# Squares for the FFN's 1/rms through PSUM and VectorE, and plain weight blocks multiplied ahead of the sums

## The chip, the cores and the metric

The kernel runs on one core of one Trainium2 chip. The metric is the device time of one execution in microseconds (us); less is better.

## The reference, cut to what matters

A trunk of two layers on x of 1024 rows by 1024 channels, float32. Each layer has a mixer, an output projection that is added to x, and then a ConvFFN that is added to x as well. Only the start of the ConvFFN is touched by the change. D_FF is 2816.

```
def rmsnorm(x, g):
    xf = x.astype(jnp.float32)
    y = xf * lax.rsqrt(jnp.mean(xf * xf, axis=-1, keepdims=True) + RMS_EPS)
    return (y * g.astype(jnp.float32)).astype(x.dtype)
...
def conv_ffn(h, w_up, w_dw, b_dw, w_down):      # h = rmsnorm(x, g_ffn[l])
    u = h @ w_up
    u = causal_dwconv(u, w_dw, b_dw)            # width 3 over the rows
    gate, val = jnp.split(u, 2, axis=-1)
    return (jax.nn.silu(gate) * val) @ w_down
```

## The kernel before

The residual x lies in SBUF transposed, as eight tiles `x[0]` to `x[7]` of 128 channels by 1024 rows (two halves `h0`, `h1` of 512). Every product is made of three matmuls with operands split in a high part (a cast on ACT) and a low part (a subtraction at L82, on POOL for weights, on DVE for many x operands).

`ffn(l)` computes the up-projection in 22 column pairs c (gate columns and value columns), and each pair by seven Strassen-like products `p1` to `p7`. A product is 12 matmuls of 128x512: four of the eight 128-deep blocks times three. Its left operand is a weight block or a sum of blocks (`A11`, `A12`, `A22` plain; `S1` to `S4` sums made on POOL by `sum1` and `sums`), its right one an x operand of `ffn_operands`: `B11`, `T1`, `B22` early, `B21`, `T2`, `T3`, `T4` by `late()`. In the trace right operands are `fB…` and `fT…` (`fT1`, `fT2`, `fT3`, `fT4` for the four T's), left ones `fwh` and `fwl`. Products add up in three kinds of PSUM banks, in program names `uX` (`p1`, then `p2`), `uV` (`p5`, then `p3`) and `uY` (`p6`, `p7`, `p4`); `uY` is one tile, `ybanks`, with a bank for even and one for odd c.

Between the products stand small steps. A copy on ACT (L522) and an add on DVE (L530, in `p5`) keep what was in the bank before the next product goes into it: `p3(c)` can't add to its V bank until L530 of c has read it, and `p2(c)` can't add to its X bank until L522 has. The factor 1/rms of each row doesn't enter the operands. It is applied afterwards: `ffn_operands` squares x and adds the squares up in `sacc`, `rstd_rows` sums over the partitions (matmuls with `ones`, L133), takes root and reciprocal (L140, L142), and spreads it over the partitions (matmuls with `ident`, L123, copied to `rb` on ACT, L506). `out2`, `out3`, `p7` and `p4` multiply by `rb`, then the convolution (L577 on ACT, L578 and L580 on DVE) and silu (L584) follow; both pairs' convolution and silu go through one PSUM tile `y`. `p4(c)` stands in the loop over columns one column late.

Before the change the first two pairs go `p1`, `late()`, the sums, `p5`, `p3`, `p2`, `p6`, `rstd_rows`, `p7`. The written order is not the order on an engine: a scheduler which simulates the program places each engine's instructions, and each engine then runs its own in that order. PSUM tiles come from rings: tag `b1` from four single banks, tag `b2` in turn from two tiles of two banks, of which `st`, `y` (b2a) and `ybanks` (b2b) are others.

The out-projection ahead of the FFN adds its result to x bank by bank (L334 on DVE); its last matmuls, tile `op`, and the first ones of the FFN share the ring of single banks.

Of the kernel before, what the change touches and what calls it, by code (L numbers as in the profile page):

```python
# [8 lines left out]
F32 = mybir.dt.float32  # L9
F32R = mybir.dt.float32r  # L10
BF16 = mybir.dt.bfloat16
AF = mybir.ActivationFunctionType
ALU = mybir.AluOpType
# [38 lines left out]
class Trunk:  # L52
# [308 lines left out]
    def ffn_operands(self, l):  # L361

        nc = self.nc
        K2 = KD // 2
        gain = f"g_ffn{l}"
        x = self.x
        h0, h1 = slice(0, HS), slice(HS, S)  # L370
        names = ("B11", "T1", "B22", "B21", "T2", "T3", "T4")
        ops = {n: ([None] * K2, [None] * K2) for n in names}
        for n in names[:3]:
            for k in range(K2):
                for i in range(2):
                    ops[n][i][k] = self.fp.tile([P, HS], F32R, tag="h2", name=f"f{n}{i}{k}", bufs=6 * K2)

        def op(n, k):
            return ops[n][0][k], ops[n][1][k]

        acc = self.main.tile([P, S], F32, tag="rb", name="sacc")
        v = nc.vector
        for k in range(K2):
            for q in (k, k + K2):
                for sl in (h0, h1):
                    nc.sync.dma_start(self.d_x[:, q, sl], x[q][:, sl])
                    if q == 0:
                        nc.scalar.activation(acc[:, sl], x[q][:, sl], AF.Square)
                    else:
                        sq = self.nt("sq")  # L390
                        nc.scalar.activation(sq, x[q][:, sl], AF.Square)
                        nc.gpsimd.tensor_tensor(acc[:, sl], acc[:, sl], sq, op=ALU.add)
            g, g2 = self.vec(gain, k), self.vec(gain, k + K2)
            x11, x12, x21, x22 = x[k][:, h0], x[k][:, h1], x[k + K2][:, h0], x[k + K2][:, h1]
            nc.scalar.activation(x11, x11, AF.Copy, scale=g)
            self.split(*op("B11", k), x11, lo_eng=v)
            v.scalar_tensor_tensor(x12, x12, g, x11, op0=ALU.mult, op1=ALU.subtract)
            self.split(*op("T1", k), x12, lo_eng=v)
            self.split_gain(*op("B22", k), x22, g2)
            v.scalar_tensor_tensor(x22, x22, g2, x12, op0=ALU.mult, op1=ALU.subtract)  # L400
            v.tensor_tensor(x11, x22, x11, op=ALU.subtract)
            v.scalar_tensor_tensor(x12, x21, g2, x22, op0=ALU.mult, op1=ALU.subtract)


        def late():
            for k in range(K2):
                for n, sl, q in (("B21", h0, k + K2), ("T2", h1, k + K2)):
                    for i in range(2):
                        ops[n][i][k] = self.htile(f"f{n}{i}{k}")
                    self.split_gain(*op(n, k), x[q][:, sl], self.vec(gain, q) if n == "B21" else None)  # L410
            for k in range(K2):
                for n, sl in (("T3", h0), ("T4", h1)):
                    for i in range(2):
                        ops[n][i][k] = self.htile(f"f{n}{i}{k}")
                    self.split(*op(n, k), x[k][:, sl], lo_eng=v)
        return ops, acc, late

    def ffn(self, l):
# [6 lines left out]
        with self.fstack:  # L425
# [20 lines left out]
            def load(c):  # L446
                if c >= NF:
                    return
                a = self.main.tile([P, KD, P], F32, tag="raw", name="wa", bufs=self.NRAW)
                nc.sync.dma_start(a, self.wup[l, c])  # L450
                if c > 1:
                    self.load_b(l, c)
                raws[c] = a, self.wbs.pop(c)
# [3 lines left out]
            def sums(c):  # L457

                a, b = raws[c]
                if c < 2:  # L460
                    s1 = first[c]
                    u = unit("s24").rearrange("p (k c) -> p k c", k=KD)
                    s2, s4 = u[:, lo4], u[:, hi4]
                else:
                    u = unit("s12").rearrange("p (k c) -> p k c", k=KD)
                    s1, s2 = u[:, lo4], u[:, hi4]
                    s4 = self.nt("s4").rearrange("p (k c) -> p k c", k=K2)
                g = nc.gpsimd
                if c > 1:
                    g.tensor_tensor(s1, b[:, lo4], b[:, hi4], op=ALU.add)  # L470
                g.tensor_tensor(s2, s1, a[:, lo4], op=ALU.subtract)
                g.tensor_tensor(s4, a[:, hi4], s2, op=ALU.subtract)
                g.tensor_tensor(b[:, lo4], a[:, lo4], b[:, lo4], op=ALU.subtract)
                st[c]["A"].update({"S1": s1, "S2": s2, "S3": b[:, lo4], "S4": s4,
                                   "A12": a[:, hi4], "A22": b[:, hi4]})

            def begin(c):

                st[c] = {"A": {"A11": raws[c][0][:, lo4]}}

            def sum1(c):
                s1 = first[c] = self.nt("s1").rearrange("p (k c) -> p k c", k=K2)
                b = raws[c][1]
                nc.gpsimd.tensor_tensor(s1, b[:, lo4], b[:, hi4], op=ALU.add)

# [15 lines left out]
            def rstd_rows():  # L501
                ps = self.ps.tile([P, 2, HS], F32, tag="b2a", name="st")
                rs = [self.rstd_cols(acc[:, hf * HS:(hf + 1) * HS], 4, D, self.eps_rms, ps[:, hf, :4])
                      for hf in range(2)]
                for hf, r in enumerate(rs):
                    nc.scalar.copy(rb[:, hf * HS:(hf + 1) * HS], self.bcast_row(r, 4, ps[:, hf]))  # L506
# [34 lines left out]
            def out2(c):  # L541
                d = st[c]
                nc.vector.tensor_tensor(d["g"][:, h0], d["X"], rb[:, h0], op=ALU.mult)
# [11 lines left out]
            def out3(c):  # L555
                d = st[c]
                V = d["V"]
                nc.vector.tensor_tensor(V, V, d["g"][:, h1], op=ALU.add)
                nc.vector.tensor_tensor(d["g"][:, h1], V, rb[:, h1], op=ALU.mult)
                d["y"] = conv(c, 0)  # L560
# [31 lines left out]
            p1(0)  # L592
            p1(1)
            late()
            for c in range(2):
                sums(c)
            for c in range(2):
                st[c]["g"] = unit("ug")
            for f in (p5, p3, p2, p6, p7):
                for c in range(2):  # L600
                    f(c)
                if f == p6:
                    rstd_rows()
                    for c in range(2):
                        out2(c)
                        out3(c)
                if f == p6:
                    load(2)
                    begin(2)
                    sums(2)  # L610
                    load(3)
            p4(0)
            for c in range(2, NF):
                for f, i in ((p1, 0), (p4, -1), (p6, 0), (p5, 0), (p2, 0), (p7, 0), (p3, 0)):
# [951 lines left out]
```

## Time and profile before

| | |
|---|---|
| time, median of 3 runs | 2364.68 us (2360.47 to 2378.05) |
| profiled execution | 2361.07 us, span 2359.3 us, mean granted clock 0.984 |
| PE busy | 2262.8 us, 96% of the span |
| DVE, ACT, POOL busy | 1472.1, 1075.9, 1380.4 us |

The profile is of one execution on the core. Busy time is that in which an engine works on an instruction; a row of the timeline names what ended the idle time before it. The first FFN begins at 426.03 us, where the last out-projection matmul ends, the second at 1651.91 us. The rows that the prediction rests on stand in a section of their own below.

### The profile page before, as it was taken

What the parts mean: (1) busy time and instruction counts of PE and PEld (TensorE: products, weight loads), DVE (VectorE), ACT (ScalarE), POOL (GpSimd) and SP (SyncE); (2) the same over time, 40 slices, a digit from 0 to 9 for tenths busy, and PEclk for the clock granted to TensorE, in tenths of its full rate; (3) what the DMA queues carried; (4) which work ended last, traced back from release to release, by engine and by line L of the source; (5) the groups of instructions that cost most, each with busy time, mean ns of one, the idle gap of its engine ahead of it and who ended that gap; (6) DMA issues with size and microseconds to landing.
All of it is one profiled execution on the core that took longest, in us unless ns stands there. A gap on an engine that the chain in (4) does not pass through costs nothing.

```text
span 2359.3 us, 29756 instructions
## 1 busy us (share of the span) xinstructions
PE 2262.8 (96%) x10970; PEld 1868.8 (79%) x10970; DVE 1472.1 (62%) x1967; ACT 1075.9 (46%) x1864; POOL 1380.4 (59%) x1031
## 2 busy tenths in 40 slices
PE   6999889899999999999998999999899999999998
PEld 6777668678788878888897888788678888778887
DVE  7479787666666664325655777866766666655225
ACT  6886745444434344122542665754444333343212
POOL 3685846677777776453423443615776868666533
PEclk9999989999999999999999999999999999999999
DMA  6101113122222235332432232433122222245322
GB/s 240 36 27 33 41 54 117 43 97 73 82 80 84 78 111 184 108 109 88 134 104 80 70 80 73 120 109 117 51 93 72 90 72 90 72 130 182 107 72 72
DMA packets 85281, 216.74 MB, mean 92 GB/s; under 512 B 9008, under 2 KB 29232, under 8 KB 85136
## 3 DMA queue, kind: packets, MB, share of 16 engines
q1 hardware_dynamic: 84992, 214.52, 28.5%
q8 instruction: 86, 1.41, 0.2%
q14 instruction: 59, 0.48, 0.1%
q10 hardware_dynamic: 144, 0.32, 0.0%
HBM read 156.94 MB, written 51.58 MB: 88 GB/s over the span
## 4 chain that ended last, share of the span: by engine, by line
PE 81%; DVE 10%; ACT 3%; issue 2%; POOL 2%; DMA 2%; DVEq 0%; ACTq 0%; POOLq 0%
PE uY L345 15%; PE uX L345 10%; PE uV L345 10%; PE dn L109 7%; PE dn L108 7%; PE dn L110 7%; PE vps L1108 3%; PE pq L108 2%; PE pq L110 2%; PE pq L109 2%; DVE fT L82 1%; PE fo L1291 1%; PE ft L1282 1%; PE fo L1290 1%; PE fs L1246 1%
## 5 line engine op out<-in xcount | busy, mean ns | idle before, releaser
L345 PE MATMUL uY<-fT,fwh 128*128 128x512 f32 x1056 | 331.1, 394 | 4.7 <-DVE fuv L547 3.2
L109 PE MATMUL dn<-gl,wd_hi 128*128 128x512 f32 (+1 forms) x752 | 284.6, 379 | 1.0 <-POOL gl L82 1.0
L108 PE MATMUL dn<-gh,wd_hi 128*128 128x512 f32 (+1 forms) x752 | 280.3, 377 | 0.0
L110 PE MATMUL dn<-gh,wd_lo 128*128 128x512 f32 (+1 forms) x752 | 278.9, 375 | 0.0
L648 DVE TENSOR_TENSOR fx<-fx,dn 128x512 f32<-128x512 f32 (+1 forms) x176 | 111.1, 637 | 262.6 <-PE dn L110 262.5
L345 PEld LDWEIGHTS uY<-fT,fwh 128*128 128x128 f32 x1056 | 196.9, 188 | 55.5 <-DVE fuv L547 9.8
L345 PE MATMUL uX<-fB,fwh 128*128 128x512 f32 x704 | 221.6, 396 | 6.4 <-ACT fuv L522 3.9
L345 PE MATMUL uY<-fT,fwl 128*128 128x512 f32 x528 | 206.7, 392 | 0.0
L82 POOL TENSOR_TENSOR wd_lo<-wd_raw,wd_hi 128x1024 fp32r<-128x1024 f32 x44 | 108.1, 2463 | 134.2 <-ACT wd_hi L81 125.4
L82 POOL TENSOR_TENSOR fwl<-wa,fwh 128x512 fp32r<-128x512 f32 x88 | 118.0, 1342 | 110.7 <-ACT fwh L81 109.7
L108 PEld LDWEIGHTS dn<-gh,wd_hi 128*128 128x128 f32 x752 | 141.1, 188 | 28.2
L345 PEld LDWEIGHTS uX<-fB,fwh 128*128 128x128 f32 x704 | 132.7, 189 | 38.6 <-ACT fuv L522 5.6
L82 POOL TENSOR_TENSOR fwl<-wb,fwh 128x512 fp32r<-128x512 f32 x88 | 119.4, 1359 | 74.5 <-ACT fwh L81 74.3
L110 PEld LDWEIGHTS dn<-gh,wd_lo 128*128 128x128 f32 x752 | 141.1, 188 | 27.1
L109 PEld LDWEIGHTS dn<-gl,wd_hi 128*128 128x128 f32 x752 | 141.3, 188 | 26.7 <-POOL gl L82 1.8
L861 POOL TENSOR_TENSOR yp<-yp,ct 128x512 f32<-128x512 f32 x100 | 135.7, 1360 | 28.4 <-ACT ct L860 23.4
L82 POOL TENSOR_TENSOR gl<-g,gh 128x512 fp32r<-128x512 f32 x88 | 117.3, 1354 | 49.1 <-ACT gh L81 49.0
L345 PE MATMUL uX<-fB,fwl 128*128 128x512 f32 x352 | 137.7, 394 | 0.0
L82 POOL TENSOR_TENSOR fwl<-fs,fwh 128x512 fp32r<-128x512 f32 x88 | 117.9, 1341 | 26.9 <-ACT fwh L81 26.9
L81 ACT CAST fwh<-wa 128x512 fp32r<-128x512 f32 x88 | 54.3, 619 | 157.7 <-PE uY L345 125.3
L345 PE MATMUL uV<-fB,fwh 128*128 128x512 f32 x352 | 111.6, 395 | 7.4 <-DVE fuv L530 7.4
L345 PEld LDWEIGHTS uY<-fT,fwl 128*128 128x128 f32 x528 | 99.4, 188 | 22.4
(398 smaller groups left out, 6287.9 us busy)
## 6 DMA issues: line engine op xcount, KB each, us to landing
wb<-in_wup SPq DMA_DIRECT2D x44, 512.0 KB
wa<-in_wup SPq DMA_DIRECT2D x44, 512.0 KB
d_g<-fsg SPq DMA_DIRECT2D x44, 512.0 KB
wd_raw<-in_wdn SPq DMA_DIRECT2D x44, 512.0 KB
g<-d_g SPq DMA_DIRECT2D x44, 512.0 KB
d_x<-x SPq DMA_DIRECT2D x32, 256.0 KB
nxs<-d_x SPq DMA_DIRECT2D x32, 256.0 KB
wia_raw<-in_wia SPq DMA_DIRECT2D x14, 512.0 KB
```

The source lines that it names most:

```text
L81: nc.scalar.copy(hi, src)
L82: (lo_eng or nc.gpsimd).tensor_tensor(lo, src, hi.bitcast(F32), op=ALU.subtract)
L108: nc.tensor.matmul(out, lhsT=ah, rhs=bh, start=start and i == 0, stop=False)
L109: nc.tensor.matmul(out, lhsT=ah, rhs=bl, start=False, stop=False)
L110: nc.tensor.matmul(out, lhsT=al, rhs=bh, start=False, stop=stop and i == n - 1)
L345: mm = nc.tensor.matmul(out, lhsT=w[:, k], rhs=h[k], start=start and k == 0 and j == 0, stop=k == n - 1 and j == 2, skip_group_check=True)
L648: return nc.vector.tensor_tensor(self.x[m][:, sl], self.x[m][:, sl], ps, op=ALU.add)
L861: nc.gpsimd.tensor_tensor(y[:, hf], y[:, hf], c, op=ALU.add)
L1108: nc.tensor.matmul(ps, lhsT=a[hf][k][:, tsl], rhs=w[:, k % 4], start=k == 0 and j == 0, stop=k == KD - 1 and j == 2)
L1246: mm = nc.tensor.matmul(o, lhsT=d["q1"][:, qs], rhs=d["k1"][:, ksl], start=True, stop=False)
L1282: mm = nc.tensor.transpose(pt[:, u, P:], p1[:, j * P:(j + 1) * P], self.ident)
L1290: nc.tensor.matmul(po, lhsT=vs[:, j], rhs=ph[:, u], start=j == 0, stop=False)
```

## The change

First, in `ffn_operands` ACT writes the squares of x (but for the first tile, which still goes to `sacc` directly) to a PSUM tile `sq`, and DVE adds them to `sacc` (L390). Before, they went to SBUF (`nsq`, L391) and POOL added them (L392). These are 14 adds in each layer. Second, in the first two pairs `p5` and `p2` are called right after `late()`, ahead of `sums`; so that they can be, `begin` registers the block `A12` and `sum1` the sum `S1`. `rstd_rows` and `out2`, `out3` stay behind `p6`.

```
@@ ffn_operands
                 sq = self.ps.tile([P, S], F32, tag="b2", name="sq")
                 for sl in (h0, h1):
                     nc.sync.dma_start(self.d_x[:, q, sl], x[q][:, sl])
-                    if q == 0:
-                        nc.scalar.activation(acc[:, sl], x[q][:, sl], AF.Square)
-                    else:
-                        sq = self.nt("sq")
-                        nc.scalar.activation(sq, x[q][:, sl], AF.Square)
-                        nc.gpsimd.tensor_tensor(acc[:, sl], acc[:, sl], sq, op=ALU.add)
+                    nc.scalar.activation(acc[:, sl] if q == 0 else sq[:, sl], x[q][:, sl], AF.Square)
+                    if q:
+                        v.tensor_tensor(acc[:, sl], acc[:, sl], sq[:, sl], op=ALU.add)
@@ ffn, begin and sum1
-                st[c] = {"A": {"A11": raws[c][0][:, lo4]}}
+                a = raws[c][0]
+                st[c] = {"A": {"A11": a[:, lo4], "A12": a[:, hi4]}}
-                s1 = first[c] = self.nt("s1").rearrange("p (k c) -> p k c", k=K2)
+                s1 = first[c] = st[c]["A"]["S1"] = self.nt("s1").rearrange("p (k c) -> p k c", k=K2)
@@ ffn, first two pairs
             late()
+            p5(0)
+            p5(1)
+            p2(0)
+            p2(1)
             for c in range(2):
                 sums(c)
...
-            for f in (p5, p3, p2, p6, p7):
-                for c in range(2):
-                    f(c)
-                if f == p6:
-                    rstd_rows()
-                    ...
+            for f in (p3, p6):
+                f(0)
+                f(1)
+            rstd_rows()
+            for c in range(2):
+                out2(c)
+                out3(c)
+            load(2)
+            begin(2)
+            sums(2)
+            load(3)
+            p7(0)
+            p7(1)
             p4(0)
```

What the change moves is seen in the engines' orders. On PE in layer 0, in the middle of the first two pairs, before (`fT_36xx` in `uY` is `T2`, `fB_348x` in `uV` is `B22`, `fB_36xx` in `uX` is `B21`; so these rows are the end of `p5`, the spreading of 1/rms, `p3`, `p2` and `p6`):

```order
L345 MATMUL uV<-fT_3486,fwl 128x512
L345 MATMUL uY<-fT_3647,fwh_3811 128x512
L345 MATMUL uY<-fT_3648,fwh_3811 128x512
L123 MATMUL st<-ident,rs 128x128 x4
L345 MATMUL uV<-fB_3488,fwh 128x512
L345 MATMUL uV<-fB_3489,fwh 128x512
L345 MATMUL uX<-fB_3643,fwh 128x512
L345 MATMUL uX<-fB_3644,fwh 128x512
L345 MATMUL uY<-fT_3647,fwl_3812 128x512
```

After, at the same place (now `fT_364x` is `T2`, `fB_366x` is `B21`), the end of `p2`, then `p6` of c0, and `p3`:

```order
L345 MATMUL uX<-fB_3661,fwl 128x512
L345 MATMUL uY<-fT_3641,fwh_3805 128x512
L345 MATMUL uY<-fT_3642,fwh_3805 128x512
L133 MATMUL st<-ones_69,sacc 128x1
L345 MATMUL uV<-fB_3488,fwh 128x512
L345 MATMUL uV<-fB_3489,fwh 128x512
L345 MATMUL uY<-fT_3641,fwl_3806 128x512
...
L345 MATMUL uV<-fB_3488,fwh 128x512
L345 MATMUL uV<-fB_3489,fwh 128x512
```

All of `p2` of both pairs now stands ahead of the first `p3` matmul, where before it stood behind; the sums of `sacc` over the partitions (L133), which stood ahead of these rows before, now stand among them.

On DVE, at the end of the out-projection of layer 0, before (`x13` and `x17` are `x[3]` and `x[7]`, the last tiles that the out-projection adds to, `op` its result in PSUM):

```order
L334 TENSOR_TENSOR x13_2773<-x13_2773,op_3382 128x512
L334 TENSOR_TENSOR x13_2773<-x13_2773,op_3402 128x512
L169 SCALAR_TENSOR_TENSOR fB2112_3660<-x16_2763,vecs_63,fB2102_3659 128x512
L82 TENSOR_TENSOR fB1113_3479<-x13_2773,fB1103_3478 128x512
L397 SCALAR_TENSOR_TENSOR x13_2773<-x13_2773,vecs_63 128x512
L166 TENSOR_TENSOR fT212_3664<-x16_2763,fT202_3663 128x512
L334 TENSOR_TENSOR x17_2765<-x17_2765,op_3428 128x512
L82 TENSOR_TENSOR fT113_3487<-x13_2773,fT103_3486 128x512
L169 SCALAR_TENSOR_TENSOR fB2113_3668<-x17_2765,vecs_63,fB2103_3667 128x512
L334 TENSOR_TENSOR x17_2765<-x17_2765,op_3448 128x512
```

After, the same place:

```order
L334 TENSOR_TENSOR x13_2773<-x13_2773,op_3382 128x512
L390 TENSOR_TENSOR sacc_3496<-sacc_3496,sq_3570 128x512
L334 TENSOR_TENSOR x13_2773<-x13_2773,op_3402 128x512
L169 SCALAR_TENSOR_TENSOR fB2112_3654<-x16_2763,vecs_63,fB2102_3653 128x512
L390 TENSOR_TENSOR sacc_3496<-sacc_3496,sq_3570 128x512
L395 SCALAR_TENSOR_TENSOR x13_2773<-x13_2773,vecs_63 128x512
L82 TENSOR_TENSOR fB1113_3479<-x13_2773,fB1103_3478 128x512
L166 TENSOR_TENSOR fT212_3658<-x16_2763,fT202_3657 128x512
L334 TENSOR_TENSOR x17_2765<-x17_2765,op_3428 128x512
L82 TENSOR_TENSOR fT113_3487<-x13_2773,fT103_3486 128x512
L390 TENSOR_TENSOR sacc_3496<-sacc_3496,sq_3577 128x512
L334 TENSOR_TENSOR x17_2765<-x17_2765,op_3448 128x512
```

Three of the adds of squares (one of them, for the first half of `x17`, is the one on `sq_3577` here) now stand between the four additions to the last two tiles of x.

Further on in DVE's queue, the splits of `T3` and `T4` (L82) and the adds that empty the V banks, before:

```order
L142 RECIPROCAL rs<-sd 128x4
L82 TENSOR_TENSOR fT_3692<-x_2771,fT_3691 128x512
L82 TENSOR_TENSOR fT_3696<-x_2771,fT_3695 128x512
L82 TENSOR_TENSOR fT_3700<-x_2773,fT_3699 128x512
L530 TENSOR_TENSOR fuv<-uV,fuv 128x512
L82 TENSOR_TENSOR fT_3704<-x_2773,fT_3703 128x512
L530 TENSOR_TENSOR fuv<-uV,fuv 128x512
```

After, where the same adds have line L529:

```order
L529 TENSOR_TENSOR fuv<-uV,fuv 128x512
L82 TENSOR_TENSOR fT_3686<-x_2771,fT_3685 128x512
L82 TENSOR_TENSOR fT_3690<-x_2771,fT_3689 128x512
L529 TENSOR_TENSOR fuv<-uV,fuv 128x512
L82 TENSOR_TENSOR fT_3694<-x_2773,fT_3693 128x512
L82 TENSOR_TENSOR fT_3698<-x_2773,fT_3697 128x512
L525 TENSOR_TENSOR fug<-uY,fuv 128x512
L142 RECIPROCAL rs<-sd 128x4
```

The add of c0 moved up past three of the eight splits and that of c1 past two, and the reciprocals (L142), of which one stood here and one ahead of the splits, stand behind all eight. At the very beginning of layer 0's FFN, too, PE's order differs: right behind the out-projection stood `p1` of c0 (`uX`); now twelve matmuls of `p5` stand there (ten of c0, two of c1, in `uV`), then `p1`. In layer 1 `p1` stands first in both.

## Rows read from the trace of the kernel before

**Rows 1.** The page, engines' busy time, and the chain that ended last.

```profile
PE 2262.8 (96%) x10970; PEld 1868.8 (79%) x10970; DVE 1472.1 (62%) x1967; ACT 1075.9 (46%) x1864; POOL 1380.4 (59%) x1031
...
PE 81%; DVE 10%; ACT 3%; issue 2%; POOL 2%; DMA 2%; DVEq 0%; ACTq 0%; POOLq 0%
```

**Rows 2.** Timeline of PE, layer 0: start us, duration us, line, op, [idle before <-releaser].

```profile
425.64 0.39 PE L110 MATMUL op<-mxh,wo_lo 128*128 128x512 f32 x1
428.49 0.88 PE L345 MATMUL uX<-fB,fwh 128*128 128x512 f32 x2 [2.46 <-DVE x L334]
...
453.39 1.19 PE L345 MATMUL uV<-fB,fwh 128*128 128x512 f32 x2 [4.42 <-DVE fuv L530]
...
473.65 0.63 PE L345 MATMUL uX<-fB,fwh 128*128 128x512 f32 x2
...
474.35 0.63 PE L345 MATMUL uX<-fB,fwh 128*128 128x512 f32 x2
...
499.55 0.39 PE L345 MATMUL uY<-fT,fwl 128*128 128x512 f32 x1
```

**Rows 3.** Timeline of PE, layer 1.

```profile
1651.52 0.39 PE L110 MATMUL op<-bmxh,wo_lo 128*128 128x512 f32 x1
...
1665.60 1.84 PE L133 MATMUL st<-ones,sacc 128*128 128x1 f32 x8 [4.19 <-ACT sd L140]
...
1679.33 0.71 PE L345 MATMUL uV<-fB,fwh 128*128 128x512 f32 x2 [3.03 <-DVE fuv L530]
...
1698.33 0.63 PE L345 MATMUL uX<-fB,fwh 128*128 128x512 f32 x2
...
1724.20 0.39 PE L345 MATMUL uY<-fT,fwl 128*128 128x512 f32 x1
```

**Rows 4.** Windows: us, busy (xcount) of PE, PEld, DVE, ACT, POOL; PEclk; DMA share; GB/s.

```profile
440.00:450.00 10.00, 6.26 (x34) 4.78 (x32) 10.00 (x8) 6.10 (x12) 10.00 (x7) 0.97 0.00 0
450.00:460.00 10.00, 6.61 (x23) 5.38 (x24) 5.61 (x6) 0.89 (x2) 10.00 (x8) 0.69 0.33 102
...
1660.00:1670.00 10.00, 5.54 (x18) 4.16 (x17) 9.93 (x7) 7.79 (x16) 10.00 (x7) 0.56 0.00 0
```

**Rows 5.** Waits of PE, 365 to 500 us: total us, times, longest.

```profile
PE uV L345 <- DVE fuv L530: 4.4, 1, 4.4
PE st L123 <- ACT fwh L81: 2.7, 1, 2.7
...
PE uX L345 <- ACT fuv L522: 1.0, 1, 1.0
```

**Rows 6.** Groups of instructions on tile sacc.

```profile
L392 POOL TENSOR_TENSOR sacc<-sacc,nsq x28: 1277/1402/1797, 371.1 to 1659.4; 128x512 f32<-128x512 f32 x28
...
  ACT nsq L391: 37.2, 14
```

**Rows 7.** Timeline of DVE, layer 0.

```profile
427.76 0.68 DVE L334 TENSOR_TENSOR x<-x,op 128x512 f32<-128x512 f32 x1
...
431.05 0.68 DVE L334 TENSOR_TENSOR x<-x,op 128x512 f32<-128x512 f32 x1
...
434.09 1.67 DVE L400 SCALAR_TENSOR_TENSOR x<-x,vecs,x 128x512 f32<-128x512 f32 x1
...
440.78 6.83 DVE L82 TENSOR_TENSOR fT<-x,fT 128x512 fp32r<-128x512 f32 x4
...
452.56 0.68 DVE L530 TENSOR_TENSOR fuv<-uV,fuv 128x512 f32<-128x512 f32 x1
```

**Rows 8.** Timeline of ACT, layer 0.

```profile
449.70 0.57 ACT L506 COPY rb<-st 128x512 f32<-128x512 f32 x1
...
472.48 1.28 ACT L584 ACT_TABLE_LOAD   x1
...
474.84 1.21 ACT L577 ACTIVATE y<-fug,vecs 128x1024 f32<-128x1024 f32 x1
...
479.71 0.58 ACT L522 COPY fuv<-uX 128x512 f32<-128x512 f32 x1
```

More of the change, by code (lines that the diff above doesn't have):

```diff
@@ L384, in ffn_operands @@
             for q in (k, k + K2):
+                sq = self.ps.tile([P, S], F32, tag="b2", name="sq")
                 for sl in (h0, h1):
                     nc.sync.dma_start(self.d_x[:, q, sl], x[q][:, sl])
-                    if q == 0:
-                        nc.scalar.activation(acc[:, sl], x[q][:, sl], AF.Square)
-                    else:
-                        sq = self.nt("sq")
-                        nc.scalar.activation(sq, x[q][:, sl], AF.Square)
-                        nc.gpsimd.tensor_tensor(acc[:, sl], acc[:, sl], sq, op=ALU.add)
+                    nc.scalar.activation(acc[:, sl] if q == 0 else sq[:, sl], x[q][:, sl], AF.Square)
+                    if q:
+                        v.tensor_tensor(acc[:, sl], acc[:, sl], sq[:, sl], op=ALU.add)
             g, g2 = self.vec(gain, k), self.vec(gain, k + K2)
@@ L598, in ffn @@
                 st[c]["g"] = unit("ug")
-            for f in (p5, p3, p2, p6, p7):
-                for c in range(2):
-                    f(c)
-                if f == p6:
-                    rstd_rows()
[L604 to L611, printed above, removed]
+            for f in (p3, p6):
[11 more added lines that the diff above has]
+            p7(1)
             p4(0)
```

## Prediction

> **What bounds the kernel now.** I read the page first. PE is busy 96% of the span and carries 81% of the chain that ended last [rows 1]; so only time in which PE stands still or runs slowly can be won, and DVE's or POOL's busy time matters only where PE waits for it. The change touches the first two column pairs of the two FFNs, so I then read PE's timeline there, from the last out-projection matmul to the first matmul of the third pair, X(2).
>
> In layer 0 that is from 425.64 + 0.39 = 426.03 to 473.65 us, 47.6 us [rows 2]. What should it take? From 473.65 to 474.35 three matmuls go through, 0.23 us each [rows 2]. By the order, 132 matmuls of the first two pairs stand in the stretch (all but 12 of the 144, `p7(1)`), 30.3 us, and I estimate 4 us for the small matmuls of `st`. So 47.6 - 34.3 = **13.3 us are lost**. Named gaps are 2.5 (for DVE's L334), 2.7 (for ACT's cast) and 4.4 us (for L530) [rows 2, 5]; the rest is slow running: the clock is 0.69 in 450 to 460 [rows 4]. In layer 1: 1651.91 to 1698.33, 46.4 us, **12.1 lost**, with gaps of 4.2 and 3.0 [rows 3], clock 0.56 in 1660 to 1670 [rows 4]. Together 25.4 us, 1.08% of 2361: the ceiling. The L530 waits are the core: `p3` may not add to its bank until DVE has emptied it, and DVE reaches that add at 452.56 only, behind the splits of T3 and T4, four of which take 6.83 us [rows 7], with DVE and POOL both 10.00 busy of 10 [rows 4].
>
> **The squares.** The POOL adds take 41.9 us (28 at 1.50; the median is 1.40), half in each layer, and POOL sits idle 37.2 us ahead of them waiting for ACT's squares [rows 6]. Removed, they free 21 us of POOL per layer, and POOL's queue is no longer held up. Nothing waits for POOL for long in layer 0, so by itself this gives PE nothing; it lets S1 and the splits of A12 be ready before the out-projection ends.
>
> DVE gets 14 adds per layer with one operand in PSUM. No such add on `sacc` is in the trace; the nearest are L334 and L530, 0.68 us each though POOL was busy beside L530 [rows 4, 7], against 1.67 to 1.71 for operations with SBUF operands alone in the same stretch [rows 7]. I take 0.68 and keep 1.7 as the upper end; below 0.68 no row shows one. 14 x 0.68 = 9.5 us per layer, of which most falls in waits of DVE during the out-projection. Three adds stand between the last additions to x, however, and hold up L334 of x17: walking the queue I get 430.8 instead of 427.76, about 3 us, and X(0) may start then, not at 428.49. At 1.7 each it would be 3 us more. ACT's squares cost 0.63 before and I take the same, so nothing.
>
> **The order of the products, layer 0.** I walked PE through the new order with the durations of before.
> - Start: twelve matmuls of p5 stand ahead of X(0), in a bank that is free, so the 2.46 us gap goes. They fill 426.03 to 428.8; then PE waits for DVE again, X(0) from 430.9. Saved here: the 12 matmuls in front, 2.8, less the delay of X(0), 2.4.
> - Then p1, p5, p2 of both pairs run without a wait to 444.6 (the operands B21 are ready). This is the point of the reorder: 24 matmuls of p2 stand in front of the L529 waits.
> - L529 of c0 and c1 now stand two and three splits earlier in DVE's queue, at about 446 and 449.3, since the adds in front push the queue by 3 us and the removal of three resp. two splits (1.7 each) pulls them by 3 to 5. PE's waits for them: 1.3 and 0.9 us in place of 2.70 + 4.42.
> - X(2) starts at 466.7 with `p7(1)` done. Before it was 473.65 with 12 matmuls to go, equivalent to 476.4: **9.7 us ahead**.
> - But `rstd_rows` is now behind p6. `rb` was ready at 449.70 + 0.57 = 450.3 [rows 8]; now only after the bcast behind `p7`, at 467.4. All that multiplies by `rb` (out2, out3, convolution, silu) begins 17 us later and comes in one lump: `p4(1)` waits for L564 of c0, which stands behind c0's convolution on DVE, 1.7 to 3.2 us; `p2(2)` waits for the copy L522 on ACT, queued behind both pairs' convolution steps (1.21 each), the table load (1.28) and silu. Before, that copy was at 479.71 and PE waited 0.98 [rows 5, 8]; now about 4 us.
> - The walk reaches the end of `p6(2)`, with the same products done, at 494.4 to 495.8, against 499.55 + 0.39 = 499.9 [rows 2]. So of the 9.7 us, 4.3 to 5.6 are given back and **4 to 5.5 us** remain.
>
> What a 4 us stall costs afterwards: after the one at 449 to 453 the clock showed 0.69 [rows 4], which would take another 0 to 1.8 us. I take a gain of 4.7 for layer 0, with ends of 1 and 8.
>
> **Layer 1.** There p1 stands first as before, and there is no L334 gap. After p2, at 1668.8, PE waits for both L529: 3.7 and 2.6 us by the walk, in place of 4.19 and 3.03 [rows 3]. X(2) starts at 1694.7 with 12 more matmuls done, but the lump behind `rb` takes most of it back: `p6(2)` ends at 1722.4 to 1723.8, before at 1724.20 + 0.39 = 1724.6 [rows 3]. **0.8 to 2.2 us**, I take a gain of 1.5, with ends of -2 and 7.
>
> The adds and the order elsewhere: from the third pair on, PE's order differs by small moves only up to about the sixteenth pair. PE is full there, so I take nothing, with 2 us per layer either way. Queues on SP keep their order; the load for pair 2 is issued earlier, 441 instead of 455, with nothing waiting behind it.
>
> **Sum.** 2361.07 - 4.7 - 1.5 = 2354.9 against the profiled execution. That stands 3.6 us under the median of the runs, and the runs lie from 2360 to 2378; a median like that of before would be 2358.5. I take **2357**.
>
> **Rivals.**
> 1. *DVE gets out of POOL's way.* Between 430 and 442 POOL has little left to do once its adds are gone and its splits are done early; then L400 to L402 and the splits take 0.7 instead of 1.7 [rows 7]. Some seven of them, 7 us of DVE, lie ahead of L529. In layer 0 X(2) would start at 463.9, and `p6(2)` gain 8; in layer 1 up to 7. 2361 - 15 = 2346. Against: POOL is 10.00 busy to 460 before [rows 4], and S2 to S4 wait for DVE and so fall together with the splits again. 0.2. The Trainium skill, "SBUF — State Buffer", section "Who interferes with whom", says that a VectorE instruction with two SBUF inputs contends with a GpSimd one that reads SBUF, and that the later blocks until the first has ended, while one with a single SBUF input doesn't contend. The 1.71 against 0.68 beside the same busy POOL agrees with it. By that rule this rival is smaller: only the three or four DVE operations that fall into a truly idle POOL get 1 us each back, 2361 - 6.2 - 4 = 2351 as an estimate, and the moved adds, with one SBUF input, never cost 1.7, so that rival 4 would fall away.
> 2. *All start losses go,* with no new wait behind `rb`: 25.4 us, 2336. It would need PE's p4 and p2 not to wait for the conv lump, which the walk contradicts. 0.05.
> 3. *Nothing is won:* the wait behind `rb` takes back all. Each us by which `rb` is later than 467.4 costs one; 4.5 us later and layer 0 is even. 2359 to 2363. 0.2.
> 4. *Slower:* the adds on DVE go at 1.7 us rather than 0.68. Then the x17 additions, L529 and `rb` are each 3 to 9 us later, layer 0 ends at 0 to +5, layer 1 at +3 to +7, and the longer stall of `p2(2)` halves the clock for a while, +2 each: 2364 to 2377, say 2370. It decides once `rb` is ready after 471.9 in layer 0. Against: L530's 0.68 beside a busy POOL. 0.13.
>
> **How the numbers follow.** My forecast, 2350 to 2360, has 0.42; it is the likeliest, and 2357 its value by the median. The range reaches over rivals 1, 3 and part of 4: 2343 to 2371. One per cent, 23.6 us, is about what a measurement can tell from no change; rival 2 passes it, and so would a run of rival 1 with luck in the runs: 0.06 faster. Slower by that much is the end of rival 4 alone, with a slow draw: 0.05. The rest, 0.89, is within it.
>
> **What would show it.** Right: no gap in front of the first FFN matmul of layer 0; an add of squares of 0.6 to 0.7 on DVE; PE gaps for L529 under 2 us each in layer 0 and of 2 to 4 in layer 1; X(2) at 465 to 468; the copy of `rb` near 467; one gap of about 4 us at `p2(2)` for ACT's L521; `p6(2)` ending near 495 and 1723. Wrong: adds above 1 us, a late L334, an out-projection that ends after 426 because L334 frees its banks late, or gaps past the third pair that were not there before.

## The result, and the profile after

The changed kernel takes **2348.6 us** (2345.69 to 2350.18, 9 runs) against 2364.68 before (2360.47 to 2378.05, 9 runs): ratio 0.9934, 95% interval 0.9923 to 0.9945. The time lies in the range and the sign is right, but the gain of 16 us is twice what the point forecast said (7.7 under the median). It ends between the two versions of rival 1 (2346 and 2351); the profiled execution, 2350.14, lies next to the second.

The profiled execution fell by 11.0 us in span, from 2359.3 to 2348.3. Between the starts of the last matmuls `op` of layer 0 and the first of layer 1 it became 6.0 us shorter (1096.2 to 1090.2), from the last `op` of layer 1 to the end 6.0 as well (707.8 to 701.7); the stretch ahead of the first FFN became 0.8 longer and the out-projection of layer 1 0.3. Both layers won alike. The other 5 us of the medians lie between profiled executions and medians: the profiled one of before is 3.6 us under its median, the one of after 1.5 above.

PE's timeline after, layer 0 (answers to [rows 2]):

```profile
426.42 0.39 PE L110 MATMUL op<-mxh,wo_lo 128*128 128x512 f32 x1
426.64 0.63 PE L345 MATMUL uV<-fT,fwh 128*128 128x512 f32 x2
...
463.61 0.71 PE L345 MATMUL uX<-fB,fwh 128*128 128x512 f32 x2
...
470.92 0.73 PE L345 MATMUL uY<-fT,fwh 128*128 128x512 f32 x2 [1.52 <-DVE fuv L564]
...
477.46 0.99 PE L345 MATMUL uX<-fB,fwh 128*128 128x512 f32 x2 [3.52 <-ACT fuv L521]
```

The first matmul of the FFN follows the out-projection without a gap. X(2) starts 37.2 us after the start of the last `op`, before 48.0 [rows 2], and with the 12 matmuls of `p7(1)` done: 10.8 + 2.8 = 13.6 us ahead, the whole loss of 13.3. Then two new gaps, 1.52 and 3.52, and behind the second the matmuls run at half pace for a while (granted clock 0.50 in 479 to 481). Layer 1 (answers to [rows 3]):

```profile
1646.59 0.39 PE L110 MATMUL op<-bmxh,wo_lo 128*128 128x512 f32 x1
...
1666.37 0.71 PE L345 MATMUL uV<-fB,fwh 128*128 128x512 f32 x2 [1.46 <-DVE fuv L529]
...
1685.77 0.71 PE L345 MATMUL uX<-fB,fwh 128*128 128x512 f32 x2
...
1693.07 0.72 PE L345 MATMUL uY<-fT,fwh 128*128 128x512 f32 x2 [1.52 <-DVE fuv L564]
...
1699.61 1.14 PE L345 MATMUL uX<-fB,fwh 128*128 128x512 f32 x2 [3.51 <-ACT fuv L521]
```

X(2) starts 39.2 us after the last `op`, before 46.8 [rows 3]: 7.6 + 2.8 = 10.4 of the 12.1 us are gained, with one wait of 1.46 for L529, and the same two gaps follow. The windows after (columns as in [rows 4]):

```profile
430.00:440.00 10.00, 10.00 (x45) 8.17 (x44) 9.92 (x12) 8.32 (x17) 6.26 (x4) 1.00 0.19 60
440.00:450.00 10.00, 10.00 (x49) 8.33 (x48) 7.11 (x8) 3.42 (x6) 10.00 (x8) 1.00 0.20 59
470.00:480.00 10.00, 5.56 (x19) 4.17 (x20) 6.11 (x8) 7.22 (x10) 0.87 (x1) 0.89 0.01 2
1660.00:1670.00 10.00, 8.54 (x38) 6.68 (x37) 9.01 (x8) 4.33 (x8) 10.00 (x6) 1.00 0.36 107
```

In 440 to 450 PE is full, at full clock, where it stood at 6.26 of 10 before, and in 1660 to 1670 it has 8.54 where it had 5.54 [rows 4]. POOL has room in 430 to 440 (6.26), and the loss has moved to 470 to 480. VectorE after (answers to [rows 7]):

```profile
379.70 0.69 DVE L390 TENSOR_TENSOR sacc<-sacc,sq 128x512 f32<-128x512 f32 x1 [0.67 <-ACT sq L388]
...
424.94 0.67 DVE L334 TENSOR_TENSOR x<-x,op 128x512 f32<-128x512 f32 x1
...
428.12 0.68 DVE L334 TENSOR_TENSOR x<-x,op 128x512 f32<-128x512 f32 x1
429.47 0.69 DVE L390 TENSOR_TENSOR sacc<-sacc,sq 128x512 f32<-128x512 f32 x1 [0.67 <-ACT sq L388]
...
430.91 0.75 DVE L398 SCALAR_TENSOR_TENSOR x<-x,vecs,x 128x512 f32<-128x512 f32 x1
...
432.31 0.74 DVE L400 SCALAR_TENSOR_TENSOR x<-x,vecs 128x512 f32<-128x512 f32 x1
...
439.33 0.68 DVE L529 TENSOR_TENSOR fuv<-uV,fuv 128x512 f32<-128x512 f32 x1
...
442.76 0.68 DVE L529 TENSOR_TENSOR fuv<-uV,fuv 128x512 f32<-128x512 f32 x1
```

L398 to L400 are L400 to L402 of before: 0.75 instead of 1.67 us [rows 7]. The add of squares takes 0.69, with POOL idle (429.47) and beside POOL at work (379.70) alike. The adds that empty the V banks end at 440.0 and 443.4; the first stood at 452.56 before [rows 7]. What POOL does meanwhile shows in its rows, after and then before:

```profile
379.23 2.55 POOL L483 TENSOR_TENSOR ns<-wb 128x512 f32<-128x512 f32 x2 [3.83 <-DMA wb<-in_wup]
...
425.09 1.30 POOL L469 TENSOR_TENSOR fs<-ns,wa 128x512 f32<-128x512 f32 x1 [3.09 <-DVE fT L166]
433.74 1.69 POOL L469 TENSOR_TENSOR fs<-ns,wa 128x512 f32<-128x512 f32 x1 [7.35 <-DVE fT L166]
```

```profile
430.53 2.98 POOL L484 TENSOR_TENSOR ns<-wb 128x512 f32<-128x512 f32 x2
...
435.17 1.74 POOL L473 TENSOR_TENSOR wb<-wa,wb 128x512 f32<-128x512 f32 x1
```

After, S1 (`ns`) is made at 379.23, and POOL stands idle for 7.35 us ahead of 433.74; before, S1 was made at 430.53, and a train of POOL work ran from there on. ACT after (answers to [rows 8]):

```profile
463.89 0.59 ACT L505 COPY rb<-st 128x512 f32<-128x512 f32 x1 [3.23 <-PE st L123]
...
469.60 1.28 ACT L583 ACT_TABLE_LOAD   x1 [3.15 <-DVE y L579]
...
471.96 1.21 ACT L576 ACTIVATE y<-fug,vecs 128x1024 f32<-128x1024 f32 x1
...
476.82 0.58 ACT L521 COPY fuv<-uX 128x512 f32<-128x512 f32 x1
```

The second half of `rb` is ready at 464.5, before at 450.3 [rows 8]. Behind it come both convolutions, table load and silu, and the copy of X(2) starts at 476.82 though X(2) itself was done at 466.7. That is the give-back.

### The profile page after: what moved, and what is told of

It is laid out like the page before. It is cut to its first block, busy times and chain, and to the rows that moved or that the text cites. A ratio compares the mean times of both kernels' runs of the same rounds, so it can differ in the third digit from the quotient of the medians.

```text
span 2348.3 us, 29697 instructions
## 1 busy us (share of the span) xinstructions
PE 2261.3 (96%) x10970; PEld 1869.1 (80%) x10970; DVE 1457.6 (62%) x1995; ACT 1075.4 (46%) x1864; POOL 1335.9 (57%) x1003
## 4 chain that ended last, share of the span: by engine, by line
PE 52%; DVE 4%; POOL 2%; issue 2%; DMA 2%; ACT 1%; DVEq 0%; ACTq 0%; POOLq 0%; SPq 0%
PE uY L345 7%; PE dn L109 7%; PE dn L108 6%; PE dn L110 6%; PE uX L345 5%; PE uV L345 5%; PE vps L1111 3%; PE pq L108 2%; PE pq L110 2%; PE pq L109 2%; DMA wd_raw<-in_wdn 1%; PE ft L1285 1%; PE fo L1294 1%; PE fo L1293 1%; PE fs L1249 1%
## 5 line engine op out<-in xcount | busy, mean ns | idle before, releaser
L82 POOL TENSOR_TENSOR fwl<-wa,fwh 128x512 fp32r<-128x512 f32 x88 | 118.7, 1350 | 119.0 <-ACT fwh L81 119.0
L82 POOL TENSOR_TENSOR wd_lo<-wd_raw,wd_hi 128x1024 fp32r<-128x1024 f32 x44 | 108.0, 2461 | 127.5 <-ACT wd_hi L81 120.5
L82 POOL TENSOR_TENSOR fwl<-wb,fwh 128x512 fp32r<-128x512 f32 x88 | 119.4, 1359 | 63.8 <-ACT fwh L81 63.0
L82 POOL TENSOR_TENSOR gl<-g,gh 128x512 fp32r<-128x512 f32 x88 | 117.0, 1350 | 56.9 <-ACT gh L81 56.7
L82 POOL TENSOR_TENSOR fwl<-fs,fwh 128x512 fp32r<-128x512 f32 x88 | 118.3, 1346 | 52.9 <-ACT fwh L81 52.9
L81 ACT CAST wd_hi<-wd_raw 128x1024 fp32r<-128x1024 f32 x44 | 45.6, 1050 | 152.4 <-issue 83.7
```

Source lines behind the costliest of these rows:

```text
L81: nc.scalar.copy(hi, src)
L82: (lo_eng or nc.gpsimd).tensor_tensor(lo, src, hi.bitcast(F32), op=ALU.subtract)
```

## The experiments

Medians are of their own group of runs; the kernel before had medians of 2370.5 us (the first four experiments), 2363.7 (the next four), 2380.4 (the next three) and 2369.5 in them, and two of these groups, 2363.7 and 2380.4, ran on the same chip. The changed kernel had 2348.6 and 2347.7 in two groups, so it is mostly before that varies, and ratios of different groups carry that with them. Traces are therefore compared by the two FFN stretches, from the start of the last `op` matmul of layer 0 to that of layer 1 and from there to the end, without what lies ahead of the first FFN. Between two traces of the changed kernel their sum differs by 0.6 us.

**squares_only.** The old order of the products with the squares of the change:

```
-                        nc.scalar.activation(sq, x[q][:, sl], AF.Square)
-                        nc.gpsimd.tensor_tensor(acc[:, sl], acc[:, sl], sq, op=ALU.add)
+                    nc.scalar.activation(acc[:, sl] if q == 0 else sq[:, sl], x[q][:, sl], AF.Square)
+                    if q:
+                        v.tensor_tensor(acc[:, sl], acc[:, sl], sq[:, sl], op=ALU.add)
```

> The squares alone: PSUM and VectorE as in the changed kernel, the old order of the products. Theory A (room beside POOL: what wins most is that VectorE's operations after the last addition to x, L398 to L400 and the split of T2, no longer run beside POOL's adds and sums): these take 0.7 instead of 1.7 us, the second add that empties a V bank is done near 445 instead of 455 in layer 0, PE's wait for it falls from 4.4 to under 2 us, and the time is 0.9935 to 0.997 of before. Theory B (the order: p2 in front of p3 covers the waits, the squares matter little): waits of 3 us or more stay in both layers, 0.998 to 1.001.

2345.85 us, 0.9897 (0.9862 to 0.9932), span 2341.8: 17.5 us under before, 2.0 of them ahead of the first FFN. The 15.5 in the two FFN stretches are more than the 11.7 of the whole change. PE has no wait for the V adds left in layer 0; its longest waits there, in the waits view (total, times, longest), are:

```profile
PE uY L345 <- DVE fuv L563: 1.8, 1, 1.8
PE st L123 <- DVE rs L142: 1.2, 1, 1.2
```

What the expectation of theory A named came about: L398 to L400 and the split of T2 take 0.68 to 0.75, and the second V add is done at 442.35. The gain is larger than it said, the whole interval lies under its 0.9935 to 0.997.

**order_only.** The new order with the squares of before (SBUF, POOL).

> The order alone: p5 and p2 of the first two pairs ahead of the sums, POOL still adds the squares. Theory A: POOL is busy from 429 to 455 in layer 0, L400 to L402 stay at 1.7 us, the adds that empty the V banks come at 450 or later, PE still waits 2 to 5 us per layer in front of p3, 0.997 to 1.000 of before. Theory B: p2 covers these waits, 0.993 to 0.996, as the whole change.

2357.96 us, 0.9937 (0.991 to 0.9965), span 2357.4. The operations are as theory A had them, in VectorE's timeline:

```profile
433.29 1.68 DVE L400 SCALAR_TENSOR_TENSOR x<-x,vecs,x 128x512 f32<-128x512 f32 x1
...
436.59 1.77 DVE L402 SCALAR_TENSOR_TENSOR x<-x,vecs 128x512 f32<-128x512 f32 x1
...
451.85 0.68 DVE L531 TENSOR_TENSOR fuv<-uV,fuv 128x512 f32<-128x512 f32 x1
```

L531 still comes at 451.85, and PE still waits 2.5 us in front of p3 and 3.1 at the start for L334. Yet the ratio is theory B's. Its trace holds one very long operation, which before_copy below prices at 7.7 us; without it the FFN stretches would be 1925.5, 8.2 less than before, an estimate. So the order alone wins as well: both A and B hold in part, and the parts don't add up in the changed kernel.

**pool_dummy.** The changed kernel, with extra work on POOL:

```
+            for i in range(5):
+                dm = self.nt("dm")
+                nc.gpsimd.tensor_tensor(dm, ops["T1"][1][K2 - 1], ops["T1"][0][K2 - 1], op=ALU.add)
             late()
```

> The changed kernel with five extra POOL additions per layer into a scratch tile, placed where POOL was idle while VectorE does L398 to L400 and the split of T2 (extra work, no result uses it). Theory A: those VectorE operations go from 0.7 to 1.6 or more, the L529 adds come 3 to 4 us later, PE waits 1 to 4 us per layer more, 2351 to 2357 us (0.9945 to 0.997 of before). Theory B, or POOL's blocking not being the cause: 2347 to 2350, as without them.

```profile
429.99 1.66 DVE L398 SCALAR_TENSOR_TENSOR x<-x,vecs,x 128x512 f32<-128x512 f32 x1
...
433.28 1.78 DVE L400 SCALAR_TENSOR_TENSOR x<-x,vecs 128x512 f32<-128x512 f32 x1
...
441.31 0.68 DVE L529 TENSOR_TENSOR fuv<-uV,fuv 128x512 f32<-128x512 f32 x1
...
444.70 0.68 DVE L529 TENSOR_TENSOR fuv<-uV,fuv 128x512 f32<-128x512 f32 x1
```

This is VectorE's timeline: three operations go from 0.7 to 1.66 to 1.78, as theory A says, so POOL beside them is the cause. The second L529 stands 20.6 us behind the start of the last `op` matmul (at 424.13 here), in the two traces of the changed kernel 16.3 and 17.3: 3.3 to 4.2 later, again as theory A says. PE's waits for it are only 1.1 us in layer 0 and 0.8 in layer 1, since p2 stands in front of p3, and the FFN stretches (1921.5) are those of the changed kernel (1921.9 and 1921.3). The median, 2356.05 (0.9928, 0.9899 to 0.9957), doesn't settle the size: its runs spread from 2344.6 to 2364.3.

**rb_early.** The changed kernel, with one call moved:

```
             p2(1)
+            rstd_rows()
             for c in range(2):
                 sums(c)
...
-            rstd_rows()
             for c in range(2):
                 out2(c)
```

> The changed kernel with the rows of 1/rms made right behind p2, ahead of p3 and p6. Theory of the give-back (the waits of 1.5 us in front of p4 and 3.5 us in front of p2 of the third pair, and the slow clock behind them, come from rb being ready only after p7): rb is ready some 10 us earlier, both waits go in both layers, 4 to 12 us less than the changed kernel, 2337 to 2345 us (0.9885 to 0.992 of before). Rival: ACT's root and table load now hold PE up in front of p3, 2347 to 2352.

2338.73 us, 0.9864 (0.9826 to 0.9901), span 2336.9. The rows of `rb` on ACT, and the only waits of PE listed in 422 to 505:

```profile
453.27 0.59 ACT L505 COPY rb<-st 128x512 f32<-128x512 f32 x1 [1.61 <-PE st L123]
...
455.78 0.59 ACT L505 COPY rb<-st 128x512 f32<-128x512 f32 x1 [0.50 <-PE st L123]
```

```profile
PE uY L345 <- DVE fuv L546: 2.3, 2, 1.5
```

`rb` is ready at 456.4 instead of 464.5 (32.3 instead of 38.1 us behind the start of the last `op` matmul), and both waits of the give-back are gone in both layers. So `rb` being late costs the changed kernel 9.1 us in the two FFN stretches (8.5 against its second trace, below): the two gaps in each layer, 2 x 5.0, and some half-clock time behind them, less the waits for L546. The other 2.3 us of the 11.4 by which the span is shorter lie ahead of the first FFN.

**after_copy.** The changed kernel, unaltered.

> The changed kernel once more, word for word, so that it stands beside the others on the same chip. If the five extra POOL additions cost what theory A says, it lies 3 us or more under the 2356 us measured with them: 2345 to 2352. If they cost nothing, 2353 to 2358.

2347.68 us (2346.7 to 2348.35), 0.9933, span 2346.6. By the expectation the five POOL additions cost 3 us or more, 2356.05 against 2347.68; but the two medians come from different groups on different chips, by ratio (0.9928 and 0.9933) they cost nothing, and by the traces nothing either. Whether they add spread is open, since the changed kernel did not run in pool_dummy's group.

**squares_rb.** squares_only, with `rstd_rows()` called ahead of the loop over `(p5, p3, p2, p6, p7)` instead of behind p6.

> The squares with the old order of the products, and the rows of 1/rms called ahead of p5. Theory A': with POOL out of the way the order of p2 and p3 has little left to cover, so this comes within 3 us of the early rows with the new order, 2336 to 2342 us. Rival (the new order is worth something of its own once rb is early): waits in front of p3 of 1 to 3 us per layer, 2342 to 2348.

2338.76 us, 0.9894 (0.9881 to 0.9908), span 2336.2, FFN stretches 1910.5, against 2336.9 and 1912.8 with the new order. Once `rb` is early, the new order is worth nothing that shows, as long as VectorE runs freely.

**rb_first.** The changed kernel, with `rstd_rows()` right ahead of `late()`.

> The changed kernel with the rows of 1/rms called right behind p1 of the first two pairs, ahead of p5 and p2. If rb was early enough behind p2, nothing more is won: 2336 to 2341 us, with the same wait of 1.5 us for L546 in layer 0. Rival: the matmuls on sacc now wait for the last add of squares, and one of the V adds comes a split later on VectorE, 2341 to 2347.

2339.77 us, 0.9903 (0.9887 to 0.9918), span 2335.3. `rb` is ready at 450.4 and nothing more is won; the waits for L546 stay (1.9 us in layer 0).

**sbuf_dve.** The changed kernel, with the squares in SBUF (`sq = self.nt("sq")`), still added by VectorE.

> The changed kernel with the squares in SBUF instead of PSUM; VectorE still adds them. If what counts is only that POOL is rid of the adds, it is as the changed kernel, 2345 to 2352 us, with adds of 0.68 us where POOL stands idle and 1.7 beside it. If PSUM as the place of one operand is needed too, adds at 1.3 to 1.7 us hold up the last additions to x by 2 us or more and the time is 2350 to 2358.

2347.08 us, 0.993 (0.9917 to 0.9942), span 2345.5: the time of the changed kernel, but not its trace. POOL's and then VectorE's timeline:

```profile
421.76 1.74 POOL L485 TENSOR_TENSOR ns<-wb 128x512 f32<-128x512 f32 x1 [9.59 <-DVE sacc L392]
```

```profile
431.41 1.67 DVE L400 SCALAR_TENSOR_TENSOR x<-x,vecs,x 128x512 f32<-128x512 f32 x1
...
1604.00 2.46 DVE L392 TENSOR_TENSOR sacc<-sacc,nsq 128x512 f32<-128x512 f32 x1 [0.74 <-ACT sacc L388]
```

POOL does no adds of squares here, and yet S1 is made at 421.76 only, held up 9.59 us by an add of VectorE's. S1 and the squares take their tiles from the same ring of three scratch buffers, `nt`. So POOL's work falls on top of VectorE's again, L400 takes 1.67, and PE waits 3.2 us in front of p3 in layer 0 and 2.1 in layer 1. That it is no slower goes with a `rb` that is ready at 458.0 here and 464.5 in the changed kernel; this was not taken apart. PSUM thus brings two things: the ring stays free for S1, and the add doesn't slow down. With the squares in SBUF eight of the 28 adds took 1.1 to 2.46 us, all beside POOL at work; with the squares in PSUM none took over 0.69.

**one_buf_rb.** squares_rb with the squares of before (SBUF, POOL adds), all 14 in one scratch buffer:

```
+        sq = self.nt("sq")
         for k in range(K2):
             for q in (k, k + K2):
...
-                        sq = self.nt("sq")
```

> The kernel with the old order and early rows of 1/rms (as squares_rb), but with the squares of before: in SBUF, added by POOL, only that all 14 share one scratch buffer, so that S1 of the first two pairs finds the other two of the ring of three free. Theory C (the ring: what held POOL up in the kernel before is that the squares took the scratch buffers that S1 needs, so S1 and what follows on POOL fell into the time of VectorE's splits): S1 is made before 400 us in layer 0, L400 to L402 take 0.7 to 0.8 us, 2337 to 2344 us (0.989 to 0.992 of before), though POOL still adds the squares. Theory A (the adds themselves on POOL are what hurts): VectorE's operations stay at 1.6 us, 2346 to 2356.

2371.84 us, 0.9972 (0.9949 to 0.9994), span 2380.4: neither theory's time. POOL's timeline, then VectorE's, then PE's longest wait:

```profile
378.66 2.55 POOL L484 TENSOR_TENSOR ns<-wb 128x512 f32<-128x512 f32 x2 [3.91 <-DMA wb<-in_wup]
...
436.17 1.28 POOL L392 TENSOR_TENSOR sacc<-sacc,nsq 128x512 f32<-128x512 f32 x1 [1.95 <-ACT nsq L391]
```

```profile
434.70 0.67 DVE L334 TENSOR_TENSOR x<-x,op 128x512 f32<-128x512 f32 x1
...
439.73 0.69 DVE L401 TENSOR_TENSOR x<-x,x 128x512 f32<-128x512 f32 x1
440.34 0.75 DVE L402 SCALAR_TENSOR_TENSOR x<-x,vecs 128x512 f32<-128x512 f32 x1
```

```profile
PE uX L345 <- DVE x L334: 5.6, 1, 5.6
```

S1 is early (378.66) and L401 and L402 take 0.69 and 0.75, as theory C has it, though POOL still adds squares (to 437.4; L400, which overlaps the last add, takes 1.66). But with one buffer ACT's squares wait for POOL's adds (3.6 us in 375 to 440, 2.8 of them at 412.94), the additions to `x17` come at 431.48 and 434.70, and PE waits 5.6 us for them. The experiment supports the ring as what sets S1's time; what a free ring is worth it can't show, since it was paid for with a queue. Three operations of 7.95 us in this trace, 7.7 us each by before_copy, make up another 23 of the 44 us by which it lies over squares_rb, an estimate.

**rb_early_dummy** and **squares_rb_dummy.** The five extra POOL additions, in rb_early and in squares_rb.

> The changed kernel with the rows of 1/rms behind p2, and the five extra POOL additions per layer of pool_dummy (extra work, no result uses it). If the new order's p2 in front of p3 covers VectorE's delay: at most 1 us of new wait per layer, 2338 to 2342 us.

> The same five POOL additions with the old order of the products and early rows of 1/rms. If the new order is a cover for a late VectorE and the old one is none: the V adds come 3 us later and p3 waits 2 to 4 us per layer, 2342 to 2348 us; if the scheduler's old order covers as well (p6 fills in): 2338 to 2342.

2340.74 us (0.9833, 0.9811 to 0.9855; span 2341.0) and 2358.47 us (0.9911, 0.989 to 0.9931; span 2359.7). The intervals don't touch. With the new order the same disturbance costs 1.7 and 1.0 us of waits for L529; with the old one PE waits 3.8 us in front of p3 in layer 0, where the clock in 440 to 450 falls to 0.66, and 1.3 us in layer 1. The waits view names a cast; but L528, which empties that bank, ends at 444.24 and the matmul starts at 444.38, so it is L528 that was waited for:

```profile
PE uV L345 <- ACT fwh L81: 3.8, 1, 3.8
```

So in layer 0 the new order covers a late VectorE, as the first theory of the expectation said. The 18 us between the medians are more than these waits: two operations of 7.95 us stand in the old order's trace, none in the new order's. Without them, an estimate by before_copy, the additions cost the old order 8.8 us of FFN stretches (squares_rb) and the new one 3.1 (rb_early). Whether the order keeps the long operations away or chance did, one trace of each can't tell; and squares_rb without the additions did not run in this group, in which before, too, was 17 us slower than in that of squares_rb.

**before_copy.** The kernel before, unaltered.

> The kernel before, word for word, profiled once more. Theory D (what spreads the times of the kernel before from 2359 to 2389 us is that now and then a multiplication by rb on VectorE, L548, is shut out for a whole train of POOL operations, 7.95 us in place of 1.3, PE then stands still 5.75 us and runs at half clock behind it, some 9 us in all): the profiled time is 2360 us plus 9 us, within 2, for each L548 of over 7 us in its trace. Rival: the trace is slower than 2366 us and has none of them.

Its profiled time is 2369.3 us, 2367.5 in span, and it holds exactly one such operation. VectorE's row, then POOL's:

```profile
759.53 7.96 DVE L548 TENSOR_TENSOR fuv<-fuv,rb 128x512 f32<-128x512 f32 x1
```

```profile
759.43 1.33 POOL L82 TENSOR_TENSOR fwl<-fs,fwh 128x512 fp32r<-128x512 f32 x1
...
765.65 1.28 POOL L470 TENSOR_TENSOR fs<-wb 128x512 f32<-128x512 f32 x1
767.01 1.59 POOL L471 TENSOR_TENSOR fs<-fs,wa 128x512 f32<-128x512 f32 x1
```

L548, with both inputs in SBUF, starts 0.1 us behind a POOL operation and ends at 767.49, 0.56 us behind the end (766.93) of the last of six POOL operations that follow without a break; POOL pauses there for 0.08 us. PE stands still for 5.76 us, until 770.06, and the clock is 0.50 in the windows from 768 to 774. In the execution of [rows 2 to 4], at 2361.07, there is none; there the same L548 also starts 0.1 us behind a POOL operation, and takes 1.78 us (the expectation has 1.3):

```profile
759.50 1.78 DVE L548 TENSOR_TENSOR fuv<-fuv,rb 128x512 f32<-128x512 f32 x1
```

The difference, 8.2 us (7.7 in the FFN stretches), is inside what theory D gave. That the times of before between 2359 and 2389 are executions with none, one or more of these fits, but only one of each kind was profiled, at 2361 and 2369.

**Side by side.** The two FFN stretches of one trace each, and the operations of over 7 us on VectorE in it:

| run | stretches, us | long operations |
|---|---|---|
| before | 1933.6 | 0 |
| squares_only | 1918.2 | 0 |
| order_only | 1933.2 | 1 |
| after, after_copy | 1921.9, 1921.3 | 0 |
| rb_early | 1912.8 | 0 |
| squares_rb | 1910.5 | 0 |

The squares alone win 15.5 us, the order alone some 8.2 when its long operation is taken out, both 11.7 to 12.3. On top of the squares the order thus costs 3.2 to 3.8 us in these traces; by the times of the runs (2343.55 to 2351.89 of squares_only, 2345.69 to 2350.18 after) the two can't be told apart. `rb` goes the same way: it is ready at 450.3 before, 458.7 in squares_only, 454.7 in order_only and 464.5 with both, and with `rb` early the order costs or wins nothing that is clear (squares_rb, rb_early).

## Why the prediction came out as it did

**What bounds the kernel, and the ceiling:** right. The 13.3 us of layer 0 and 10.4 of the 12.1 of layer 1 were won at X(2).

**A reading of before.** The 2.70 us in front of the small matmuls L123 were put down to ACT's cast, as the view names it. L123 reads `rs`, and VectorE's reciprocal L142, which makes it, stood behind the first splits and ended at 447.70, 0.14 us ahead of L123 (the cast ended there too). So this wait, as well as the 4.42 us, was most likely VectorE's queue. The walk also says that the adds L529 stand two and three splits earlier; by the orders it is three for c0 and two for c1.

**The squares.** "By itself this gives PE nothing" was wrong, and it is the main mis-sized term. I counted POOL's freed time, but walked VectorE's queue at 1.67 to 1.75 us as before. With S1 made 51 us earlier POOL stood idle where VectorE worked, and squares_only shows that the squares alone take 15.5 us off the two FFN stretches. How much of it is the free ring, how much POOL's freed time, was not taken apart; pool_dummy shows that POOL at work slows the three operations from 0.7 to 1.7 us, and that under the new order this costs PE 2 us of waits at most. Rival 1 named this mechanism with its price (2346) and got 0.2; what spoke against it, POOL's 10.00 of 10, was at least in part POOL work that had been held up: S1 was made at 430.53 before, and sbuf_dve shows it waiting 9.59 us for the ring. I read the diff for operations and overlooked which buffers the removed ones had used.

**The adds on VectorE:** 0.68, as taken; they cost nothing on the path. The delay of 3 us of L334 on `x17` did not come: it stood at 424.94 and 428.12, before at 427.76 and 431.05 [rows 7].

**The order, layer 0.** X(2) was forecast at 466.7 and came at 463.61, 37.2 us behind the start of the last `op` matmul where the forecast had 41.1 and rival 1 (463.9) 38.3. The give-back was forecast at 1.7 to 3.2 and 4 us and measured 1.52 and 3.52; its cause, `rb` ready at 467.4 by the walk and at 464.5 in the trace, is shown by rb_early. Net 6.0 instead of 4.7. The walk priced the order with VectorE as slow as before, and order_only, which comes closest to that case, won some 4.4 in layer 0 and 3.8 in layer 1 against 4.7 and 1.5, though there `rb` was early and nothing was given back.

**Layer 1** is the size that was off most: 6.0 instead of 1.5. The waits for L529, forecast at 3.7 and 2.6, were 1.46 and none, again because VectorE was not slowed.

**Sum and rivals.** 12 instead of 6.2 us by the layers, inside the range. That it came so near is partly luck: the sum gave the whole gain to the order and nothing to the squares, while in the runs the squares alone won more than both, and the order on top of them gave some of it back through `rb`. Rival 3 (all given back) and rival 4 (adds at 1.7) fell. The Trainium skill, "SBUF — State Buffer", section "Who interferes with whom", would have made rival 1 smaller, 2351, since only three or four operations would be freed; the trace has just these at 0.7 (L398 to L400 and the split of T2), in both layers, so the rule picked the right operations, and its 2351 lies 0.9 us from the profiled execution. The sum behind it, 6.2 for the order and 4 for the operations, is not what the runs showed, so that this too is partly luck. The page's other statement, that an instruction with one SBUF input doesn't contend, agrees with L390's 0.69 beside POOL's S1 (379.70).

**The 16 us of the medians against 11 of the profiles.** The executions of before spread over 18 us, those of after over 4.5. before_copy shows one thing that lengthens executions of before by 8 us. Neither trace of the changed kernel has it; that the changed kernel has it less often is suggested by this and by its narrow spread, and not shown.

What stays open: why the scheduler spreads 1/rms so differently when `rstd_rows` is called behind p6 each time (`rb` ready at 450.3 before, 464.5 after), and what decides that a train of POOL operations shuts VectorE out in one execution and not in the next.

**The best version** is the change with `rstd_rows()` called behind `p2(1)`: 2338.73 us, 0.9864 of before (0.9826 to 0.9901). It is as fast as the old order with early rows, and with five more POOL additions it was the faster one (2340.74 against 2358.47).

## What to carry to other kernels

When an operation is moved to another engine, ask which buffers its old form took from a shared ring, and who waited for them: here the old form held S1 back from 379 to 430 us, into VectorE's busiest time. When work is pulled forward, look at what was in its place; the small matmuls of 1/rms lost theirs, and some 9 us with it. And look at the spread of the runs: a kernel that stands close to a conflict of two engines shows it in some executions only.

## What the runs showed of the hardware

A VectorE multiplication of 128x512 with both inputs in SBUF (L548 and its like, 44 in each trace) took 0.68 to 1.84 us in the trace of before. Where POOL was at work when it started, with at least 0.2 us to go, it ended 0.55 us behind the end of the POOL operation then running (0.545 to 0.554 in that trace). The Trainium skill, "SBUF — State Buffer", section "Who interferes with whom", says that the port pair which the two engines share is an exclusive lock and that issue order decides who blocks; these times agree with it.

Seven times, in four of the 14 traces (before_copy and order_only 1, squares_rb_dummy 2, one_buf_rb 3), it took 7.94 to 7.96 us instead, while POOL ran six operations of 1.3 us one behind another. Here the wait was not for one instruction but for the first pause in POOL's train. PE stood still for 5.75 to 5.77 us each time; in before_copy its matmuls then ran at a granted clock of 0.50, the 1.2 GHz level, to about 774. The changed kernel has a shorter one:

```profile
791.71 3.59 DVE L547 TENSOR_TENSOR fuv<-fuv,rb 128x512 f32<-128x512 f32 x1
```

It lasted through three POOL operations, as in rb_early and rb_first, and PE did not wait for it.
